# Writing each loaded row to SBUF in four pieces in an interleave kernel on one core

## The chip, the core and the metric

One core of a Trainium2 chip. The metric is the device time of one execution in microseconds (us); the median of several runs is given. A second source is a profile of one execution, whose span begins with the first instruction that the profiler shows and ends with the last event.

## The reference

```
batch, seq, dim = 32, 256, 1024
result = np.zeros((batch, seq, dim * 2), dtype=np.float32)
result[..., 0::2] = x
result[..., 1::2] = y
```

Two float32 arrays of 33.55 MB each are woven together: every second element of the output comes from x, the others from y. Nothing is calculated. 67.11 MB are read and 67.11 MB are written.

## The kernel before

Both inputs are taken as one flat run of numbers, cut into n = 8 tiles of 128 partitions x 8192 elements (W). One partition's part of a tile is a row of 32 KiB that is contiguous in DRAM. The output of one tile is twice as large, so each tile has two halves h = 0 and 1: a half of the input row (H = 4096 elements) gives an output row of 8192 elements, 32 KiB.

SBUF holds two buffers each for x (`xt`), y (`yt`) and the woven halves (`ot`), each 32 KiB per partition (lines 23 to 25). Three engines each run their own list:

- SP issues all loads (lines 42 to 53). The first x tile is loaded in two halves of 16 KiB rows (lines 42 and 43), every other tile in one DMA of 128 rows of 32 KiB (4096 KB). From tile 2 on, SP first waits until the weave has read the buffer that the load will overwrite: for x at line 48, for y at line 51, both on the semaphore `woven`.
- VectorE (DVE) weaves. For each tile and half it copies 4096 elements per partition of x into the even places of `ot` (line 67) and 4096 of y into the odd ones (line 70). Before the x copy it waits for the load and, from tile 1 on, for the store that last read this `ot` buffer (`osem`).
- ACT issues the stores (lines 72 to 85), one of 4096 KB for each half, when both copies of the half are done. The very first store is cut in two, 1024 KB and 3072 KB (rows of 8 KiB and 24 KiB).

Loads go through SP's DMA queue, q1 in the profile, and stores through ACT's, q10. Both queues feed the same 16 DMA engines. `tile_interleave_kernel` moves the first two loads ahead into the program's opening block.

Of the kernel before, what the change touches and what calls it, by code (L numbers as in the profile page):

```python
# [3 lines left out]


def _interleave(nc, x, y, out):
    P = 128
    W = 8192
    H = W // 2  # L10

    total = 1
    for s in x.shape:
        total *= s
    n = total // (P * W)
    assert n * P * W == total

    def rows(ap, names, k):
        flat = ap.rearrange("b s d -> (b s d)")
        return flat[k * names : (k + 1) * names].rearrange("(p w) -> p w", p=P)  # L20

    fp32 = mybir.dt.float32
    xt = [nc.alloc_sbuf_tensor(f"xt{b}", [P, W], fp32).ap() for b in (0, 1)]
    yt = [nc.alloc_sbuf_tensor(f"yt{b}", [P, W], fp32).ap() for b in (0, 1)]
    ot = [nc.alloc_sbuf_tensor(f"ot{b}", [P, W], fp32).ap() for b in (0, 1)]

    xsem = [nc.alloc_semaphore(f"xsem{b}") for b in (0, 1)]
    hsem = nc.alloc_semaphore("hsem")
    qsem = nc.alloc_semaphore("qsem")
    ysem = [nc.alloc_semaphore(f"ysem{b}") for b in (0, 1)]  # L30
    woven = nc.alloc_semaphore("woven")
    osem = [nc.alloc_semaphore(f"osem{b}") for b in (0, 1)]


    cuts = [0, W // 4, W]
    parts = [slice(a, b) for a, b in zip(cuts, cuts[1:])]

    xs = [rows(x, P * W, k) for k in range(n)]
    ys = [rows(y, P * W, k) for k in range(n)]
    os_ = [rows(out, 2 * P * W, k) for k in range(n)]  # L40

    nc.sync.dma_start(out=xt[0][:, :H], in_=xs[0][:, :H]).then_inc(xsem[0], 16)
    nc.sync.dma_start(out=xt[0][:, H:], in_=xs[0][:, H:]).then_inc(hsem, 16)

    for k in range(n):
        b = k % 2
        if k >= 2:
            nc.sync.wait_ge(woven, 4 * (k - 2) + 3)
        if k:
            nc.sync.dma_start(out=xt[b], in_=xs[k]).then_inc(xsem[b], 16)  # L50
        if k >= 2:
            nc.sync.wait_ge(woven, 4 * (k - 2) + 4)
        nc.sync.dma_start(out=yt[b], in_=ys[k]).then_inc(ysem[b], 16)

    for k in range(n):
        b = k % 2
        for h in (0, 1):
            c = slice(h * H, (h + 1) * H)
            if h == 0:
                nc.vector.wait_ge(xsem[b], 16 * (k // 2 + 1))  # L60
            elif k == 0:
                nc.vector.wait_ge(hsem, 16)
            if k:
                nc.vector.wait_ge(osem[h], 16 * k)
            if (k, h) == (1, 0):
                nc.vector.wait_ge(qsem, 16)
            nc.vector.tensor_copy(out=ot[h][:, 0::2], in_=xt[b][:, c]).then_inc(woven, 1)  # L67
            if h == 0:
                nc.vector.wait_ge(ysem[b], 16 * (k // 2 + 1))
            nc.vector.tensor_copy(out=ot[h][:, 1::2], in_=yt[b][:, c]).then_inc(woven, 1)  # L70

    for k in range(n):
        for h in (0, 1):
            nc.scalar.wait_ge(woven, 4 * k + 2 * h + 2)
            if (k, h) == (0, 0):
                for c in parts[:-1]:
                    nc.scalar.dma_start(
                        out=os_[k][:, c], in_=ot[h][:, c]
                    ).then_inc(qsem, 16)
                c = parts[-1]  # L80
                nc.scalar.dma_start(out=os_[k][:, c], in_=ot[h][:, c]).then_inc(osem[h], 16)
                continue
            nc.scalar.dma_start(
                out=os_[k][:, h * W : (h + 1) * W], in_=ot[h]
            ).then_inc(osem[h], 16)

    nc.scalar.wait_ge(osem[0], 16 * n)
    used = sorted(s.num for s in [*xsem, hsem, qsem, *ysem, woven, osem[0]])
    assert used == list(range(used[0], used[-1] + 1)), used
    nc.scalar.sem_clear(range(used[0], used[-1] + 1))  # L90
    nc.sync.nop(nofuse=True).wait_op(osem[1], 16 * n, "sem-ge").then_inc(
        osem[1], -16 * n
    )


def kernel(tc, x, y, out):
    nc = tc.nc
    tc.close()
    tc.compile()

    _interleave(nc, x, y, out)

    blocks = nc.main_func.blocks
    for engine in (mybir.EngineType.SP, mybir.EngineType.SP):
        opening = blocks[0].instructions
        at, moved = next(
            (b, i)
            for b in blocks[1:]
            for i in b.instructions
            if i.engine == engine and i.opcode == "DMACopy"  # L110
        )
        assert not (moved.sync_info and moved.sync_info.on_wait)
        body = at.instructions
        body.remove(moved)
        gate = next(
            n
            for n, i in enumerate(opening)
            if i.engine == engine and i.opcode == "Drain"
        )
        opening.insert(gate, moved)  # L120
        at.instructions = body
        blocks[0].instructions = opening


# [1 line left out]
_INS = ['x', 'y']  # L126
_OUTS = [((32, 256, 2048), 'float32')]


# [23 lines left out]
```

## Time and profile before

| what | us |
|---|---|
| three runs | 314.19, 314.22, 314.39; median 314.22 |
| span of the profiled execution | 312.9 |
| DVE busy | 72.0 (23% of the span), 32 copies of about 2.29 |
| POOL busy | 0.2 |
| DVE idle before line 67, ended by a store | 206.5 |
| moved by the DMA engines | 134.22 MB, mean 429 GB/s |

No time of its own is given for the profiled execution besides its span; the median of the runs is 1.3 us longer than the span, which is what lies around it. DVE is mostly idle, and its idle time ends with stores that land, so the DMA side is where the time is. In the profile's DMA rows a "packet" is one record of one DMA engine: usually one row.

### The profile page before, as it was taken

How to read it: one execution, taken by the hardware profiler on the slowest of the kernel's cores; microseconds unless marked ns; L12 is line 12 of the kernel's file. 1: busy time of each engine (PE TensorE's matmuls, PEld its weight loads, DVE VectorE, ACT ScalarE, POOL GpSimd, SP SyncE). 2: the span in 40 equal slices, each digit the busy share in tenths (PEclk: the TensorE clock that was granted, in tenths of full speed). 3: DMA queues.
4: the chain of work that ended last, by engine and by line, in shares of the span. 5: the costliest groups of instructions: out<-in, count | busy, mean ns of one | idle time of the engine just before them, and what ended most of it. 6: DMA issues, size and time to landing. Idle time of an engine off the chain costs nothing.

```text
span 312.9 us, 114 instructions
## 1 busy us (share of the span) xinstructions
DVE 72.0 (23%) x32; POOL 0.2 (0%) x4
## 2 busy tenths in 40 slices
DVE  0216000501305023050220503205032050415410
POOL 0000000000000000000000000000000000000000
DMA  8999999999999999999999999999999999999998
GB/s 337 467 402 436 436 402 419 452 457 415 427 444 411 461 402 469 402 469 402 469 402 465 406 440 432 423 448 402 469 402 469 402 469 402 469 402 448 423 423 381
DMA packets 4896, 134.22 MB, mean 429 GB/s; under 512 B 544, under 2 KB 544, under 8 KB 544
## 3 DMA queue, kind: packets, MB, share of 16 engines
q1 hardware_dynamic: 2448, 67.11, 50.1%
q10 hardware_dynamic: 2448, 67.11, 49.7%
HBM read 67.11 MB, written 67.11 MB: 429 GB/s over the span
## 4 chain that ended last, share of the span: by engine, by line
DMA 82%; DVE 12%; issue 0%
DMA out_dram<-ot 76%; DMA yt<-in_y_dram 6%; DVE ot L70 6%; DVE ot L67 6%
## 5 line engine op out<-in xcount | busy, mean ns | idle before, releaser
L67 DVE COPY ot<-xt 128x4096 f32<-128x4096 f32 x16 | 36.7, 2295 | 213.8 <-DMA out_dram<-ot 206.5
L70 DVE COPY ot<-yt 128x4096 f32<-128x4096 f32 x16 | 36.6, 2288 | 12.3 <-DMA yt<-in_y_dram 12.3
L137 POOL MEMSET const-bfloat16-1.0<- 128x1 bf16 x1 | 0.1, 103 | 0.0
L137 POOL MEMSET const-uint8-127<- 128x1 uint8 x1 | 0.1, 102 | 0.0
L137 POOL MEMSET const-float32-0.0<- 128x1 f32 x1 | 0.1, 100 | 0.2 <-issue 0.2
L137 POOL MEMSET const-float32-1.0<- 128x1 f32 x1 | 0.1, 99 | 0.0
## 6 DMA issues: line engine op xcount, KB each, us to landing
out_dram<-ot ACTq DMA_DIRECT2D x15, 4096.0 KB, 34.1
yt<-in_y_dram SPq DMA_DIRECT2D x8, 4096.0 KB, 41.5
xt<-in_x_dram SPq DMA_DIRECT2D x7, 4096.0 KB, 24.3
xt<-in_x_dram SPq DMA_DIRECT2D x2, 2048.0 KB, 9.5
out_dram<-ot ACTq DMA_DIRECT2D x1, 3072.0 KB, 32.8
out_dram<-ot ACTq DMA_DIRECT2D x1, 1024.0 KB, 16.3
```

The source lines that it names most:

```text
L67: nc.vector.tensor_copy(out=ot[h][:, 0::2], in_=xt[b][:, c]).then_inc(woven, 1)
L70: nc.vector.tensor_copy(out=ot[h][:, 1::2], in_=yt[b][:, c]).then_inc(woven, 1)
L137: nc = _bacc.Bacc("TRN2", target_bir_lowering=False, num_devices=1)
```

## The change

The loads are issued by a helper that gives the source as one piece per partition and the destination as several pieces. The x and y tiles become 4 quarters (S = 4) of 2048 elements (G), each followed by 8 elements (32 bytes) that stay empty, so that the quarters are not adjacent in SBUF. A row of 32 KiB is then read as one run and written as four runs of 8 KiB (the halves of the first x tile: 16 KiB, as two runs of 8 KiB). The copies on DVE read two quarters where they read one half, and write the same places as before. The stores, the semaphores, the waits and the order of all instructions stay.

```diff
+def _split_copy(engine, out, in_):
+
+    return engine.add_instruction(
+        mybir.InstDMACopy(
+            mode="Copy",
+            name=engine.bass.get_next_instruction_name(),
+            engine=engine.engine,
+            ins=engine.lower_ap_dma(in_.rearrange("p (o w) -> p o w", o=1)),
+            outs=engine.lower_ap_dma(out),
+            queue=QUEUES[engine.engine],
+        )
+    )
...
+    S = 4
+    G = W // S
...
-    xt = [nc.alloc_sbuf_tensor(f"xt{b}", [P, W], fp32).ap() for b in (0, 1)]
-    yt = [nc.alloc_sbuf_tensor(f"yt{b}", [P, W], fp32).ap() for b in (0, 1)]
+    xt = [
+        nc.alloc_sbuf_tensor(f"xt{b}", [P, S, G + 8], fp32).ap()[:, :, :G]
+        for b in (0, 1)
+    ]
+    yt = [
+        nc.alloc_sbuf_tensor(f"yt{b}", [P, S, G + 8], fp32).ap()[:, :, :G]
+        for b in (0, 1)
+    ]
...
-    nc.sync.dma_start(out=xt[0][:, :H], in_=xs[0][:, :H]).then_inc(xsem[0], 16)
-    nc.sync.dma_start(out=xt[0][:, H:], in_=xs[0][:, H:]).then_inc(hsem, 16)
+    _split_copy(nc.sync, xt[0][:, : S // 2], xs[0][:, :H]).then_inc(xsem[0], 16)
+    _split_copy(nc.sync, xt[0][:, S // 2 :], xs[0][:, H:]).then_inc(hsem, 16)
...
-            nc.sync.dma_start(out=xt[b], in_=xs[k]).then_inc(xsem[b], 16)
+            _split_copy(nc.sync, xt[b], xs[k]).then_inc(xsem[b], 16)
...
-        nc.sync.dma_start(out=yt[b], in_=ys[k]).then_inc(ysem[b], 16)
+        _split_copy(nc.sync, yt[b], ys[k]).then_inc(ysem[b], 16)
...
-            c = slice(h * H, (h + 1) * H)
+            c = slice(h * S // 2, (h + 1) * S // 2)
+            pairs = ot[h].rearrange("p (s w two) -> p s w two", s=S // 2, two=2)
...
-            nc.vector.tensor_copy(out=ot[h][:, 0::2], in_=xt[b][:, c]).then_inc(woven, 1)
+            nc.vector.tensor_copy(out=pairs[:, :, :, 0], in_=xt[b][:, c]).then_inc(woven, 1)
...
-            nc.vector.tensor_copy(out=ot[h][:, 1::2], in_=yt[b][:, c]).then_inc(woven, 1)
+            nc.vector.tensor_copy(out=pairs[:, :, :, 1], in_=yt[b][:, c]).then_inc(woven, 1)
```

## The prediction

> **What bounds the kernel now.** I read the page first: who is busy.
>
> ```profile
> span 312.9 us, 114 instructions
> ...
> DVE 72.0 (23%) x32; POOL 0.2 (0%) x4
> ...
> DMA  8999999999999999999999999999999999999998
> ...
> q1 hardware_dynamic: 2448, 67.11, 50.1%
> q10 hardware_dynamic: 2448, 67.11, 49.7%
> ```
>
> VectorE works 23% of the span. The DMA row is at nine tenths or more in all slices but the first and last. The loads (q1) take 50.1% of the time of 16 engines and the stores (q10) 49.7%, together 99.8%. So the 16 engines are full, and a waiting VectorE costs nothing. The chain of waits and the list of who waited say the same:
>
> ```profile
> 115.55 2.29 DVE ot L67
> 117.85 2.21 DVE ot L70
> 120.06 0.02 issue
> 120.08 34.17 DMA out_dram<-ot
> 154.25 0.02 issue
> 154.28 2.29 DVE ot L67
> ```
>
> ```profile
> DVE ot L67 <- DMA out_dram<-ot: 206.5, 14, 29.0
> DVE ot L70 <- DMA yt<-in_y_dram: 12.3, 1, 12.3
> DVE ot L67 <- DMA xt<-in_x_dram: 7.3, 1, 7.3
> ```
>
> The reader should not take the 4.5 us of VectorE in each round of the chain for time that could be saved: while it weaves, the engines work on the other half's store and on loads. The windows by stage show it; the last two columns are the DMA share and GB/s.
>
> ```profile
> 60.00:100.00 40.00, 10.26 (x5) 0.00 (x0) 1.00 1.00 433
> 100.00:140.00 40.00, 9.80 (x5) 0.00 (x0) 1.00 1.00 433
> 140.00:180.00 40.00, 8.99 (x4) 0.00 (x0) 1.00 1.00 433
> 180.00:220.00 40.00, 8.99 (x4) 0.00 (x0) 1.00 1.00 433
> ```
>
> Share 1.00 and 433 GB/s in every window. Only the time of a packet can change the end, or a gap between packets.
>
> **The price of a packet.** I then went through the trace's packet records. On one engine packets follow each other without a gap, loads and stores in turn. The distance from one start to the next (medians, which in the steady stage most records meet within 1 ns) is 1209.4 ns for 32 KiB, 908.2 for 24 KiB, 607 for 16 KiB and 305.9 for 8 KiB. Steps of 8 KiB cost 1209.4 - 908.2 = 301.2 ns, that is 27.2 bytes per ns on each engine, and what is left of the 8 KiB packet is 305.9 - 301.2 = 4.7 ns. So a packet costs 301.2 ns per 8 KiB plus 4.7 ns once, for loads and stores alike. Bytes alone, 134.22 MB over 16 engines at 27.2, take 308.4 us; no version that moves these bytes at this rate is under that.
>
> **The change part by part.**
>
> *Write pieces.* An engine gets 8 of a load's 128 rows. It loads 16 tiles (8 of x, 8 of y): 15 of them in 8 rows of 32 KiB, the first x tile in 16 rows of 16 KiB: 136 rows, written so far as 136 pieces. After the change these are 128 x 4 = 512 pieces of 8 KiB: 376 more. No record shows a row that is read in one piece and written in four, so I bound it. From below, nothing: if the 4.7 ns belong to the read, or to the pair, 376 pieces add 0. Below nothing, if the 4.7 ns belonged to the end of a long write that a short one doesn't have, 136 x 4.7 = 0.64 us would go. From above, each piece costs as much as a whole 8 KiB packet, which in the records has one read and one write: 376 x 4.7 = 1.77 us. I take the upper price, 1.77 us, since 8 KiB pieces written on the same engines are the nearest row and the only one with that piece size. It is on the path that sets the end: the engines have no free time, so all of it shows.
>
> The Trainium skill speaks against this choice. Its page "DMA: Bandwidth & Descriptors", section "Why small descriptors are slow (HBM only)", puts a fixed overhead of about 3 cycles on each packet between an engine's read and write halves. The 4.7 ns found here are of that size (the trace agrees as to size; no run shows for which half it is due). By the rule, with the packet taken as the one read, the sum would be 0 instead of 1.77 us; that case is the first rival.
>
> *Where the pieces lie.* With 32 empty bytes behind each quarter, the quarters start 8224 bytes apart and the second buffer 32896 bytes after the first, so the eight quarters of a pair of buffers begin at all eight multiples of 32 within 256 bytes. Before, all pieces began at multiples of 32 KiB apart. No row of before has such a start. Nothing is the lower bound, and the value I take in the sum; the upper one is the third rival's.
>
> *Loads issued by SP.* 17 DMAs, as before, in the same order and behind the same waits. An issue takes 0.33 us, the first 0.37 us. Four times the pieces could make it longer; bounded by nothing and by one more issue, 0.37 us. Only the first one has nothing to hide it (its first packet starts between 1.0 and 1.2 us of the span); later ones lie beneath 24 to 41 us from issue to landing. I take 0 and keep 0.4 us for the range.
>
> *Copies on VectorE.* 32 copies of 2.29 us, now over two runs of 2048 in place of one of 4096. Even at twice the time a half would take 9 us, against 14.75 to 14.98 us of waiting for a store before most of them. The cover is the other half's store, which has some 19.3 us of packets left then. I take 0. If that cover were gone, each added us would cost 1 us at 15 places.
>
> *Memory and waits.* No wait is added or moved, and the stores keep their rows.
>
> Sum: 312.9 + 1.8 = 314.7 us of span. The median of the runs is 314.22, 1.3 us above the span, which I carry over: **316.0 us**, 0.56% slower.
>
> **The rivals.**
>
> *The pieces are free (not slower).* The engine reads a row as one packet and only changes the write address three times in it, under the stream of data. For it: the windows give the same 433 GB/s, and one kind of packet follows another without a gap, so addresses are made ready early. Against it: nothing in the records separates the read's part of the 4.7 ns from the write's. Price 0, so 314.2 us. It decides if a write piece's own cost is under 0.6 us / 376 = 1.7 ns.
>
> *A little faster.* The 4.7 ns of a load row vanish: 314.2 - 0.64 = 313.6 us. Against it: more pieces would have to cost less than fewer. I see no other source of gain, since engines are full from 3 us on and 308.4 us is the floor.
>
> *Start addresses cost beats.* A 32-byte step of an engine takes 301.2 / 256 = 1.18 ns. If a piece that starts within a 256-byte block also spends the steps ahead of it in that block, the eight quarters lose 0 to 7 steps, 3.5 on average: 512 x 3.5 x 1.18 = 2.1 us on top of the pieces' price, 318.1 us. For it: starts of this kind are new here. Against it: the empty steps carry no data, and a write need not move them. The Trainium skill states such a rule in "DMA: Bandwidth & Descriptors", section "How a descriptor splits into AXI transactions": a descriptor that doesn't start on a 256-byte boundary fetches from the boundary below and pays those beats. It speaks of reading; no run here shows it yet.
>
> *The change doesn't do what it says, and the load is cut on both sides.* Packets of 8 KiB alone cost the same 1.77 us. But the two queues take turns by packet (load, store, load, store in the records), so loads would get 8 KiB for each 32 KiB of stores while both wait. Stores would drain and loads come last. VectorE's y copy of the last tile (2.3 us) and the way from issue to first packet (about 1.1 us) would then find empty engines: 316.0 + 3.4 = 319.4 us. It decides when loads fall behind by more than their lead: a y tile issued at 120.08 lands about 41.5 us later, at 161.6, and is copied at 175.96.
>
> **How the numbers follow.** Pieces at packet price, 316.0: 0.45. Pieces free, 314.2: 0.25. Faster, 313.6 or less: 0.15. Start addresses, 318.1: 0.10. Cut on both sides with loads last, 319.4: 0.05. Slower by over 0.2% (0.6 us, about what a measurement of this kernel can tell from no change): 0.45 + 0.10 + 0.05 = 0.60; within it 0.25; faster by more 0.15. The likeliest case's own range is 315.2 to 316.5, from half a piece's price to the longer first issue. For 8 in 10 it goes down to 313.6, the whole of what a load row's 4.7 ns can give, and up to 318.2, the start addresses; what is left out is the last case and the outer part of the faster one.
>
> **What would show it.** Right: one round of the chain, 154.28 less 115.55 = 38.7 us for 16 load rows and 16 store rows per engine, grows by 16 x 3 x 4.7 = 0.23 us; the steady windows fall from 433 to about 430 GB/s; q1's share of the engines rises and q10's stays; a 32 KiB load packet takes 14 ns more than a store packet, or shows as four of 306 ns. Pieces free: load packets stay at 1209 ns. Start addresses: load packets differ by buffer, the second of x and y longer by some 19 ns than the first. Cut on both sides: the last load lands much later than before and the DMA row dips before its end. The forecast is wrong altogether if engines show gaps, if VectorE waits for loads in the middle, or if a packet takes less than 1209 ns.

## The result, and the profile after

Five runs of the changed kernel took 316.55 to 316.92 us, median 316.65, against 314.22 before: 2.43 us more, ratio 1.0079 with a 95% interval of 1.0068 to 1.0090. The forecast was 316.0 us, in a range of 313.6 to 318.2. The profiled execution is the longest of the five (316.92 us, span 315.6), 2.7 us above that of before, so sums made on the two profiles come out some 0.3 us higher than the medians.

The page of the changed kernel, the same lines as those shown of before:

```profile
span 315.6 us, 114 instructions
...
DVE 72.0 (23%) x32; POOL 0.2 (0%) x4
...
DMA  8999999999999999999999999999999999999997
...
DMA packets 4896, 134.22 MB, mean 425 GB/s; under 512 B 544, under 2 KB 544, under 8 KB 544
...
q1 hardware_dynamic: 2448, 67.11, 50.1%
q10 hardware_dynamic: 2448, 67.11, 49.3%
```

VectorE's 72.0 us are unchanged and the DMA row is as full as before. The count of packets is also that of before, 4896: a row that is read once is still one record, of 32 KiB, however many pieces it is written in. Now the round in the chain of waits (start, duration, what):

```profile
116.91 2.29 DVE ot L96
119.21 2.21 DVE ot L99
121.42 0.02 issue
121.44 34.52 DMA out_dram<-ot
155.96 0.02 issue
155.98 2.30 DVE ot L96
```

The same round (line 96 was line 67) takes 155.98 - 116.91 = 39.07 us where it took 154.28 - 115.55 = 38.73, and all of the difference is in the DMA's part, 34.52 against 34.17 us. The rounds that follow take 39.03, 39.08 and 39.01. The list of who waited and the windows:

```profile
DVE ot L96 <- DMA out_dram<-ot: 208.3, 14, 28.9
DVE ot L99 <- DMA yt<-in_y_dram: 12.6, 1, 12.6
DVE ot L96 <- DMA xt<-in_x_dram: 7.8, 1, 7.8
```

```profile
60.00:100.00 40.00, 9.88 (x6) 0.00 (x0) 1.00 1.00 427
100.00:140.00 40.00, 9.95 (x5) 0.00 (x0) 1.00 1.00 431
140.00:180.00 40.00, 9.93 (x5) 0.00 (x0) 1.00 1.01 433
180.00:220.00 40.00, 9.07 (x5) 0.00 (x0) 1.00 1.01 432
```

VectorE waits for the same transfers as often as before. The engines are still busy all the time (share 1.00 to 1.01) and move a little less in it, 427 to 433 GB/s where 433 stood throughout. A window counts whole packets by their start, so single figures scatter.

The trace's packet records show which packets grew. The means, of 32 KiB rows in the last 12 loads, which all run beside stores; of the first y tile, which runs before any store; and of stores:

| record, ns | before | after |
|---|---|---|
| load rows beside stores | 1213 | 1225 to 1231 |
| load rows without stores (first y tile) | 1213 | 1246 |
| half rows of the first x tile, second half (16 KiB) | 611 | 612 |
| store rows | 1213 | 1215 |

The records don't name their engine; set end to start, they fall into 16 chains. From one start to the next in a chain, a load followed by a store went from 1209.4 to 1224.1 ns (+14.7), a store followed by a load from 1209.4 to 1211.9 (+2.5). 16 such pairs in a round give 16 x 17.2 = 0.28 of the 0.34 us.

The five rounds up to the copy at 273.10 us (270.45 before) hold 1.62 of the 2.7 us between the two profiles. Another 1.03 us lies ahead of them (that chain's copy at 77.86 us was at 76.83), in tiles that load with few stores beside them and in the start. The windows at the start show the first packets, in the kernel before between 1.0 and 1.2 us:

```profile
1.00:1.20 0.20, 0.00 (x0) 0.00 (x0) 1.00 3.30 655
```

and in the changed kernel between 1.4 and 1.6:

```profile
1.40:1.60 0.20, 0.00 (x0) 0.00 (x0) 1.00 3.31 655
```

### The profile page after: what moved, and what is told of

The parts are those of the page before. It is cut to its first block, busy times and chain, and to the rows that moved or that the text cites. A ratio compares the mean times of both kernels' runs of the same rounds, so it can differ in the third digit from the quotient of the medians.

```text
span 315.6 us, 114 instructions
## 1 busy us (share of the span) xinstructions
DVE 72.0 (23%) x32; POOL 0.2 (0%) x4
## 2 busy tenths in 40 slices
DMA packets 4896, 134.22 MB, mean 425 GB/s; under 512 B 544, under 2 KB 544, under 8 KB 544
## 3 DMA queue, kind: packets, MB, share of 16 engines
q1 hardware_dynamic: 2448, 67.11, 50.1%
## 4 chain that ended last, share of the span: by engine, by line
DMA 82%; DVE 12%; issue 0%
DMA out_dram<-ot 76%; DMA yt<-in_y_dram 6%; DVE ot L99 6%; DVE ot L96 6%
```

## The experiments

The theory after the result: each extra write piece of a load takes engine time, as forecast, and the new form of the load takes longer to issue, which delays the first packet. Rivals: the displaced start addresses; the gaps; the form alone; and, against "a piece costs what a packet costs", that the price hangs on the direction or on how many pieces share a read. Medians are compared, and most kernels' runs lie within 0.15 us of their median.

**Gaps of 256 bytes.** In the tiles `G + 8` becomes `G + 64`.

> As the changed kernel, but each quarter is followed by 64 empty elements (256 bytes) in place of 8, so all pieces start at multiples of 256 bytes from each other. Piece price (each extra write piece costs some 5 ns of its engine): nothing changes, 316.6 us, load packets of about 1228 ns. Start addresses (a piece that starts within a 256-byte block costs extra steps): the load packets return to 1213 ns and only the later start of the first packet is left, 314.6 us. Pieces free and only the issue longer: 316.6 us would be unexplained.

Measured 316.63 us (316.58 to 316.68), ratio to before 1.0076 (1.0064 to 1.0089), the last tiles' load rows 1227 to 1228 ns. Nothing changes: displaced start addresses cost no extra steps.

**No gap.** `G + 8` becomes `G`; the quarters touch, and are still named as four.

> As the changed kernel without the empty elements: the four quarters of a row lie next to each other in SBUF and are still named as four. Price of a write piece, wherever it lies: 316.6 us, load packets of some 1228 ns. Price of the gap, or pieces joined again when they touch: load packets of 1213 ns, and 314.6 us, the later start alone.

Measured 316.62 us, ratio 1.0075 (1.0060 to 1.0089), load rows 1227 to 1228 ns. The gap has no price. With a gap of 32 bytes the rows of the first pair of buffers took some 1230 ns and those of the second 1225; with no gap or 256 bytes that difference is gone, and rows of both take 1225 to 1228. So where pieces lie moves 5 ns between buffers and nothing in the sum.

**The form without the pieces.** The kernel before, its loads issued by the helper with three-dimensional patterns on both sides, one piece each:

```diff
-            ins=engine.lower_ap_dma(in_.rearrange("p (o w) -> p o w", o=1)),
-            outs=engine.lower_ap_dma(out),
+            ins=engine.lower_ap_dma(in_.rearrange("p (o w) -> p o w", o=1)),
+            outs=engine.lower_ap_dma(out.rearrange("p (o w) -> p o w", o=1)),
```

> The kernel before with its loads issued by the new helper, each row as one piece in the reading and in the writing, no gaps, but with patterns of three dimensions, one of them of size 1. Form costs issue time, pieces cost engine time: issue 0.54 us, first packet later by some 0.4 us, all load packets of 1213 ns, 314.6 us. If the issue goes by the pieces: 0.33 us and 314.2 us. If all of the cost came from the form: 316.6 us.

Measured 314.54 us (one of eleven runs at 315.52), ratio 1.0012 (1.0003 to 1.0020); load rows 1213 ns in every tile after the start. This is the new form's own cost, 0.3 us, and it is the base from which the pieces are counted below. The issue took 473 ns and not the 540 expected, and the first packet came at 1.32 us of the span, against 0.99 before and 1.42 in the changed kernel. So some 0.1 us of the later start comes only with more than one piece in a row of the first load, and stands among the pieces' cost below.

**The first two loads plain.** As the changed kernel, but:

```diff
-    _split_copy(nc.sync, xt[0][:, : S // 2], xs[0][:, :H]).then_inc(xsem[0], 16)
-    _split_copy(nc.sync, xt[0][:, S // 2 :], xs[0][:, H:]).then_inc(hsem, 16)
+    nc.sync.dma_start(out=x0[:, :H], in_=xs[0][:, :H]).then_inc(xsem[0], 16)
+    nc.sync.dma_start(out=x0[:, H:W], in_=xs[0][:, H:]).then_inc(hsem, 16)
```

> As the changed kernel, but the first two loads (the halves of the first x tile) are issued in the old form, one run on both sides, and the first x tile lies without gaps. Later start caused by the longer issue of the first load (0.54 in place of 0.33 to 0.37 us) and nothing else: the first packet starts between 1.0 and 1.2 us of the span again and the time is 316.65 - 0.4 = 316.2 us. If the start is later for another reason, or is made up for later: 316.6 us.

Measured 316.30 us (316.19 to 316.32), ratio 1.0064 (1.0051 to 1.0077): 0.35 us below the changed kernel. Its windows at the start:

```profile
1.00:1.20 0.20, 0.00 (x0) 0.00 (x0) 1.00 3.73 737
```

The first packets are back between 1.0 and 1.2 us. So the later start is the first load's form, shown from both sides: 0.30 us put in, 0.35 taken out. (This kernel also has 16 write pieces per engine fewer, by estimate under 0.1 us.) The issue grows with the form, and once more when a row has more than one piece, but not with the number of pieces beyond two. The x loads' issues (the three figures behind the colon: minimum, median, maximum in ns) in the kernel before:

```profile
L50 SPq DMA_DIRECT2D xt<-in_x_dram x7: 327/328/430, 2.3 to 234.1; - x7
```

with the form without the pieces:

```profile
L15 SPq DMA_DIRECT2D xt<-in_x_dram x9: 472/473/595, 0.0 to 234.4; - x9
```

in the changed kernel:

```profile
L15 SPq DMA_DIRECT2D xt<-in_x_dram x9: 539/540/623, 0.0 to 236.4; - x9
```

and with two pieces in a row, below:

```profile
L15 SPq DMA_DIRECT2D xt<-in_x_dram x9: 539/540/607, 0.0 to 234.7; - x9
```

With eight pieces the median is 540 ns too, and 602 ns where a row is cut on both sides. The helper and its three-dimensional pattern came together, so which of the two makes the first step, from 328 to 473 ns, is not told apart. All later issues lie beneath transfers.

**Two and eight pieces.** `S = 2` (16 KiB each; the half rows whole) and `S = 8` (4 KiB each).

> As the changed kernel with S = 2: rows written in two pieces of 16 KiB, the first x tile's half rows in one piece. 120 write pieces more per engine than before, where the change has 376. Piece price, with (316.65 - 314.22 - 0.4) / 376 = 5.4 ns for each: 314.2 + 0.65 = 314.9 us. Start addresses: only one piece in two is displaced, about a third of the cost, 314.8 us: not told apart from the piece price here. A price that sets in only when a row has more than two pieces (the half rows of the changed kernel, two pieces of 8 KiB, show packets of 611 ns as before): 314.2 us.

> As the changed kernel with S = 8: rows written in eight pieces of 4 KiB. 888 write pieces more per engine than before. Piece price 5.4 ns each: 314.2 + 4.8 + 0.4 or more for the longer issue = 319.4 to 320 us, load packets of some 1250 ns. Start addresses with the displacement alone counting: offsets 0 to 224 in steps of 32 within each row, twice the pieces at the same mean price, about the same. Descriptors prepared too slowly (a limit by pieces per time): well above 320 us, with the packets of loads alone longest.

Measured 314.98 us (ratio 1.0025, 1.0015 to 1.0035) and 319.58 us (1.0169, 1.0155 to 1.0183). Above the form's 314.54 us:

| kernel | more pieces per engine | us above 314.54 | ns a piece | load row without stores | beside stores |
|---|---|---|---|---|---|
| two | 120 | 0.44 | 3.7 | 1213 | 1213 to 1217 |
| four (the change) | 376 | 2.11 | 5.6 | 1246 | 1225 to 1231 |
| eight | 888 | 5.04 | 5.7 | 1273 | 1244 to 1246 |

The time grows with the pieces. But the rows that run without stores are not on a line: 0 ns for the first extra piece, 33 for three, 60 for seven. Counted from the kernel whose first two loads are plain, whose start is nearly that of before, 316.30 - 314.24 = 2.06 us over 360 pieces is 5.7 ns; by taking the 0.1 us of the start off the 2.11 us it is 5.3. So a price per piece is good to some 0.4 ns.

**Stores in four pieces.** The kernel before with its 15 large stores in the new form; each row read from SBUF in one piece and written to DRAM in four:

```diff
-            nc.scalar.dma_start(
-                out=os_[k][:, h * W : (h + 1) * W], in_=ot[h]
+            _split_copy(
+                nc.scalar,
+                os_[k][:, h * W : (h + 1) * W].rearrange("p (s w) -> p s w", s=4),
+                ot[h],
             ).then_inc(osem[h], 16)
```

> The kernel before with plain loads, and with the 15 stores of 4096 KB in the new form: each row is read from SBUF in one piece and written to DRAM as four pieces of 8 KiB that touch. 15 x 8 x 3 = 360 more write pieces per engine. Price of a write piece of an engine, whatever the memory: 360 x 4.7 = 1.7 us, 315.9 us, store packets of some 1228 ns. Price of writing SBUF alone: 314.2 us, store packets of 1213 ns. No share of a later start in either, since the first load is as before.

Measured 314.79 us, ratio 1.0018 (1.0009 to 1.0027); store rows 1217.3 ns in the mean, 4.3 more. 0.55 us over 360 pieces is 1.5 ns each. The last three stores run beside no load, and their rows take 1218.9 ns, 5.9 more than before. Neither expectation holds: a write piece of a store costs something, but a quarter of a load's. One price for every write piece is refuted.

**Cut on both sides.** As the changed kernel, each piece with a read of its own:

```diff
-            ins=engine.lower_ap_dma(in_.rearrange("p (o w) -> p o w", o=1)),
+            ins=engine.lower_ap_dma(in_.rearrange("p (s w) -> p s w", w=2048)),
```

> As the changed kernel, but the loads read each row in four pieces of 8 KiB too, so that each piece has its own read. Piece price as that of a whole packet, 4.7 ns (the step of the prediction): packets of 306 ns, 376 x 4.7 = 1.8 us plus the issue, 316.4 us or more. If the price in the changed kernel comes from one read being spread over several writes: below it, 314.6 to 316.2 us. Turns by packet: loads get 8 KiB for each 32 KiB of stores and lag; the last load lands later than at 277 us of the span and the time goes to 319 us.

Measured 326.57 us, ratio 1.0389 (1.0374 to 1.0403). The packets are cheap: 309 ns in the median record, as for 8 KiB in the kernel before, and 313 in the first y tile, which runs without stores. There four of them, at 308.8 ns from start to start, take 1235 ns, a little less than one row read in one piece and written in four (1242). The loss comes from the turns: set end to start, the records run store, load, store, load while stores are queued, and after that some 40 to 50 loads in a row with no store between them. Who waited:

```profile
DVE ot L99 <- DMA yt<-in_y_dram: 112.4, 8, 15.3
DVE ot L96 <- DMA xt<-in_x_dram: 109.1, 7, 17.6
DVE ot L96 <- DMA out_dram<-ot: 15.0, 1, 15.0
```

VectorE now waits for loads in every tile, and for a store once. The windows near the end (DMA share and GB/s last):

```profile
280.00:290.00 10.00, 2.29 (x1) 0.00 (x0) 1.00 0.96 411
290.00:300.00 10.00, 0.00 (x0) 0.00 (x0) 1.00 0.67 283
300.00:302.00 2.00, 0.29 (x1) 0.00 (x0) 1.00 0.04 16
302.00:304.00 2.00, 2.00 (x2) 0.00 (x0) 1.00 0.00 0
```

The last load lands at about 301.7 us, the engines run partly empty from 290 us on and wholly around 302, and the last stores come after that. Of the 12.0 us by which its span (324.9) exceeds that of before, some 8 are engines without a packet: 8.2 us per engine between the records in their chains, against 0.1 before. (The packet times summed over 16 engines grow by 317.0 - 312.1 = 4.9 us, but records in a chain overlap, in this kernel by 2.1 us per engine and in the one before by 0.9, which is counted twice in that sum.)

**The same with even turns.** The 15 large stores are cut into 8 KiB on both sides as well.

> As the kernel whose loads are cut on both sides (326.6 us), but the 15 stores of 4096 KB are cut into pieces of 8 KiB on both sides as well, so that a turn is worth as much on either queue. If the 10 us beyond the packet price came from turns by packet: loads keep up again, no wait of VectorE for loads in the middle, and the time is 314.2 + 0.4 + (376 + 360) x 4.7 ns = 318.1 us. If they came from the loads' small reads themselves: 326 us or more.

Measured 318.26 us, ratio 1.0126 (1.0112 to 1.0140). Who waited:

```profile
DVE ot L110 <- DMA out_dram<-ot: 152.0, 14, 18.5
DVE ot L113 <- DMA yt<-in_y_dram: 69.3, 8, 13.8
DVE ot L110 <- DMA xt<-in_x_dram: 7.9, 1, 7.9
```

8.3 us come back by adding 360 packets per engine to the stores, about what the empty engines had cost. One part of the expectation failed: VectorE still waits for y in all eight tiles, 69.3 us in all, and the last load ends at 291.7 us where it ended at 276.2 before. So loads still fall behind, but the engines are full to the end (0.1 us without a packet), and the waits cost nothing. That the small reads lost by turns is shown, and so is the packet price: (318.26 - 314.54) / 736 = 5.1 ns for a packet cut on both sides, near the 4.7 read off the records.

**Two pieces for each read.** Rows of 32 KiB read in two pieces of 16 KiB and written in four, or in two for comparison; large stores cut at 16 KiB on both sides in both kernels.

> As the changed kernel with four write pieces of 8 KiB in a row, but two reads of 16 KiB for them, so two pieces for each read; the 15 stores of 4096 KB are cut at 16 KiB on both sides, so that the turns stay even. To be compared with half16base, which has one write for each such read. 256 write pieces more per engine than there. A fixed price per write piece of loads, 4.8 ns: 1.2 us above half16base. A price that sets in beyond two pieces for one read: 0 to 0.4 us above it, and load packets of 611 ns where loads run alone.

> Loads read in two pieces of 16 KiB and written in two, with 8 empty elements between them; the 15 stores of 4096 KB in two pieces of 16 KiB on both sides. 120 + 120 packets more per engine than before, at 4.7 ns each, and the later start: 314.2 + 1.1 + 0.4 = 315.7 us; by the prediction's price of a packet all of it shows. If turns or the gaps matter as well, more.

Measured 316.73 us (ratio 1.0077, 1.0065 to 1.0090) and 316.01 us (1.0054, 1.0040 to 1.0068). The difference, 0.72 us over 256 pieces, is 2.8 ns a piece: between the two expectations, so it decides neither. The base itself is 0.3 us above what 4.7 ns a packet gives. In loads without stores (the third to fifth group of 128 such records) the 16 KiB reads with two pieces took 619 to 626 ns in the mean against 611 with one; the half rows at the start of the changed kernel had shown 612. So two pieces per read are not free in general.

**The cost alone.** One profiled execution of a kernel that only copies, stage by stage, on SP's queue. Windows by stage, in the order DRAM to SBUF plain and split, SBUF to SBUF plain and split, SBUF to DRAM plain and split, DRAM to DRAM plain and split:

> The disputed cost by itself. No weaving: this kernel leaves out the whole interleave and only copies, on SP's queue, with a wait between stages, each way of copying first plain (one write piece per row) and then in four pieces of 8 KiB: DRAM to SBUF, SBUF to SBUF, SBUF to DRAM, DRAM to DRAM, rows of 32 KiB. So far a piece more in a row costs some 11 ns in loads that run alone and 1.2 to 1.7 ns in stores. If the dearer price lies in writing SBUF: DRAM to SBUF and SBUF to SBUF show split packets some 30 ns longer, the other two some 5 ns. If it lies in reading DRAM in one piece for several writes: DRAM to SBUF and DRAM to DRAM some 30 ns, the other two some 5 ns. If only the pair of the two makes it: DRAM to SBUF alone 30 ns. If a piece has one price everywhere, 14 ns in all four.

```profile
0.00:23.00 23.00, 0.20 (x4) 1.00 0.87 365
23.00:46.00 23.00, 0.00 (x0) 1.00 0.88 365
46.00:78.00 32.00, 0.00 (x0) 1.00 0.92 262
78.00:110.00 32.00, 0.00 (x0) 1.00 0.92 262
110.00:151.00 41.00, 0.00 (x0) 1.00 0.95 409
151.00:192.00 41.00, 0.00 (x0) 1.00 0.96 409
192.00:245.00 53.00, 0.00 (x0) 1.00 0.95 317
245.00:299.00 54.00, 0.00 (x0) 1.00 0.96 311
```

| 32 KiB records, mean ns after the first 64 of a stage | plain | split |
|---|---|---|
| DRAM to SBUF | 1213 | 1242 |
| SBUF to SBUF | 1838 | 1834 |
| SBUF to DRAM | 1218.2 | 1217.7 |
| DRAM to DRAM | (64 KiB records, 3195) | 1638 |

DRAM to SBUF again shows some 30 ns for three extra pieces, and stores alone show none. That differs from the 5.9 ns in the last stores of the kernel above; here the plain stores already take 1218 ns instead of 1213, for a reason that no run shows. The other two pairs are slower for another reason (1.6 to 1.8 us a row), and what is slower than the engine's own rate can hide a price of 30 ns. So "the dear price only in the pair of a DRAM read and SBUF writes" fits, but whether the DRAM side or the SBUF side makes it stays open.

## Why the prediction came out as it did

**What bounds the kernel** held: engines full, VectorE idle, and every ns of a packet came out at the end. The round of the chain grew by 0.34 us against 0.23 forecast. Of the signs named, q1's share did not rise (50.1% in both profiles), because the span it is a share of grew too; in time, the load records of an engine went from 156.5 to 158.0 us and the store records from 155.3 to 155.6.

**The write pieces.** The forecast took 1.77 us, the price of a whole 8 KiB packet for each of 376 pieces; measured above the form's own cost it is 2.11 us, 5.6 ns a piece against 4.7. Direction and size are right, and load rows beside stores grew by 14.7 ns where 14.1 were forecast; that stores beside them grew by 2.5 was not. The reason given for the size is not right: the row it was read from was an 8 KiB store, and a piece more in a store costs 1.5 ns; in loads without stores it is 0 ns for one more piece and 11 each for three. What a packet costs and what a write piece costs are two things, and that they are about alike in this kernel's steady stage is not explained by the runs. It is left open, and so far as the runs show it is luck that this term came out near.

**The Trainium skill's fixed overhead per packet** ("DMA: Bandwidth & Descriptors", section "Why small descriptors are slow (HBM only)", about 3 cycles) would be 3.5 ns if a cycle is the 1.18 ns of a 32-byte step, which is an estimate. The packets cut on both sides cost 4.7 to 5.1 ns here, so the order agrees and the size does not. The page doesn't give the price of several writes under one read, which its wording, read with the packet as the read, would put at nothing.

**The issue.** Taken as 0 with 0.4 us kept for the range: it cost 0.30 to 0.35 us, the one term that was placed wrongly, and about half of the 0.65 us by which the forecast was short; the pieces' 0.34 us are the other half. The bound was right; the value should have been taken from it, since the text itself said that the first issue has no cover. The issue itself grew by only 0.25 us (370 to 615 ns), the first packet came 0.43 us later; why it is more than the issue is not shown.

**Start addresses** (taken as 0; rival at 318.1): refuted, three gaps give 316.62 to 316.65 us. The rule of the Trainium skill, "DMA: Bandwidth & Descriptors", section "How a descriptor splits into AXI transactions", that a displaced start costs beats (the 32-byte steps), does not show for these writes; it speaks of reads, which no run here displaced.

**Pieces free, or a little faster:** refuted; load rows of 1225 ns and more.

**Cut on both sides:** the change does what it says, 4896 packets. As a mechanism the turns are real, and dearer than forecast: 326.6 us where 319.4 stood. The forecast priced only the last tile's copy and issue (3.4 us) and took the engines to be full until then; they ran partly empty from 290 us on. VectorE waited for loads in every tile, but with even turns it waited for y in every tile too, at no cost.

**VectorE and memory:** copies of 2.29 us as before, no new wait.

**Two figures of the working** are slightly off, and nothing hangs on them: 0.6 us over 376 pieces is 1.6 ns, not 1.7, and half a piece's price ends at 315.1 us, not 315.2.

No version tried here beats the kernel before.

## What to carry to other kernels

Where the DMA engines are full, count packets and write pieces: each had a small price here, of 1.5 to 5.7 ns, and all of it showed at the end. Of the pieces tried, 4 to 32 KiB, the longest on both sides were best. If one queue's rows are cut, cut the other's alike or leave both: the queues here took turns by packet, and the one with the smaller reads fell behind. Of issue costs only the first was bare, so the first load should have the plainest pattern.

## What the runs showed of the hardware that was not expected

- A write piece costs by direction: 1.5 ns in stores, 3.7 to 5.7 ns in loads, and, with four pieces in a row, more in loads that run without stores (33 ns a row) than beside them (14). With two pieces of 16 KiB a load row without stores took no longer than with one.
- An issue by SP took 328 ns with the plain pattern, 473 with the three-dimensional one and one piece in a row, 540 with two, four or eight pieces, and 602 with rows cut on both sides. With eight pieces in a row, one issue early on held SP for 9.73 us (the timeline of that kernel: start, duration, engine, line):

```profile
3.15 1.01 SPq L15 DMA_DIRECT2D xt<-in_x_dram  x1
4.20 9.73 SPq L15 DMA_DIRECT2D yt<-in_y_dram  x1
```

  It lay beneath transfers already queued and cost nothing visible.
- SBUF to SBUF ran at 1.83 us for a 32 KiB row and 262 GB/s in its stage, slower than either DRAM to SBUF (1.21 us) or SBUF to DRAM (1.22 us).
